# Transposing the FFN's hidden activations with VectorE and DMA in place of TensorE

## The chip, the core and the metric

The kernel runs on one core of a Trainium2 chip, as one program in one launch. The metric is device time in microseconds. The engines are named TensorE (PE in the profile; its weight loads are PEld), VectorE (DVE), ScalarE (ACT), GpSimd (POOL) and SyncE (SP), which issues most DMAs.

## The reference, cut to what matters

256 tokens of 1024 channels in float32 go through a first block (FFN, mixer of chunked attention and pooling, FFN, norm) and then a second block of two attention mixers with layer norms. The change concerns the two FFNs alone:

```python
def swiglu_ffn(x, w_gate, w_up, w_down):
    return (jax.nn.silu(x @ w_gate) * (x @ w_up)) @ w_down
...
x = x + 0.5 * swiglu_ffn(rmsnorm(x, ffn1_norm[l]), ffn1_w_gate[l], ffn1_w_up[l], ffn1_w_down[l])
x = x + hybrid_mixer(...)
x = x + 0.5 * swiglu_ffn(rmsnorm(x, ffn2_norm[l]), ffn2_w_gate[l], ffn2_w_up[l], ffn2_w_down[l])
```

The hidden width is 2816. The product of gate and up, called h here, is the left operand of the product down. TensorE contracts over partitions, so h, which is computed with tokens on the partitions, is needed with hidden channels on the partitions: it has to be transposed.

## The kernel before, in words

There are two tiles t of 128 tokens. Every float32 product is made of three matmuls on operands split into a high and a low part (`mm` at L161, `half` at L213): low x high, high x low, high x high, each 128x128 by up to 512 columns.

Weights come in 236 units of mostly two k-tiles by 512 columns (512 KB). SyncE loads a unit into one of four buffers `raw` (L208), ScalarE casts it to `whi` (L195) and VectorE subtracts to get `wlo` (L196); there are eight buffers of each, so a cast waits until TensorE has finished with the unit eight places earlier. `prefetch` (L184) issues these. `half` does one unit for one tile of tokens: six matmuls for a usual unit.

An FFN (`ffn`, L360 and on) goes over six blocks j of hidden channels, five of 512 and one of 256. In each block, `chunk` (L328) makes the gate product: four units for tile 0, then the same four for tile 1, 24 matmuls each. When a tile is complete, ScalarE makes `th`, a tanh (L383), and VectorE `a` (L385). Then `chunk` makes the up product in the same way, and when a tile is complete VectorE makes `h` (L392). `put_T` (L265) transposes h: one TensorE transpose for each 128x128 block into a PSUM bank `tr` (L177), then ScalarE casts the bank to the high part `hh` (L237) and VectorE subtracts for the low part `hl` (L238). In a block of 512 channels that is four transposes for each tile of tokens. After the six blocks comes the product down: two halves of 512 output columns, eleven units each, unit by unit with both tiles; unit i reads the k-tiles 2i and 2i + 1 of h.

In the first FFN, the first gate product is made by `first_chunk` (L300) with eight units of one k-tile, as the loads arrive.

The order of the work is set in two places. In the code, pieces wait in a heap with a due time in microseconds of TensorE's modelled work: `later` puts a piece in, and `pump`, at the end of every `half`, runs what is due. The h transposes are due `DUE["ffn_T"]` = 2.66 after h. Then the library that builds the program orders each engine's instructions by when it expects their operands, so an instruction can stand ahead of others that the code issues earlier; on the chip each engine runs its list in order.

GpSimd does little in an FFN: the power for the norm (L281), once for each tile, in the first gate product. It issues one DMA in the whole program, the load of `gain` (L1076).

Of the kernel before, what the change touches and what calls it, by code (L numbers as in the profile page):

```python
# [16 lines left out]
P = 128  # L17
# [18 lines left out]
# column blocks of the products with x on the left, in the order in which they are used  # L36
FFN_CH = [(512 * j, min(512, DFF - 512 * j)) for j in range((DFF + 511) // 512)]
MIX_CH = [(1536, 512), (512, 512), (0, 512), (1024, 512)]           # u k q v
FOX_CH = [(1024, 512), (1536, 512), (0, 512), (512, 512),           # k0 k1 q0 q1
          (0, 344), (344, 344), (688, 344),                          # of [f | v]  # L40
          (3080, 512), (3592, 512)]                                  # gate
DSA_CH = [(0, 372), (372, 372),                                      # of [ki | qi | wi | kr | ckv]
          (0, 512), (512, 512), (1768, 512), (2280, 512)]            # q gate


def unit_list():
    """(matrix, first k-tile, k-tiles, first column, columns) in the order of use."""
    u = []

    def block(m, c0, w, k0=0, k1=KT, n=None):  # L50
        n = n or (UK * (512 // w) if 512 % w == 0 else UK)
        for k in range(k0, k1, n):
            u.append((m, k, min(n, k1 - k), c0, w))

    def ffn(i):
        for c0, w in FFN_CH:
            block(f"gate{i}", c0, w, n=1 if i == 1 and c0 == 0 else None)
            block(f"up{i}", c0, w)
        for n in range(2):
            block(f"down{i}", 512 * n, 512, 0, FT)  # L60

    ffn(1)
    for c0, w in MIX_CH:
        block("mix", c0, w)
    for k0 in (4, 0):
        for n in range(2):
            block("mix_out", 512 * n, 512, k0, k0 + 4)
    ffn(2)
    for i, (c0, w) in enumerate(FOX_CH):
        block("fox_fv" if 4 <= i < 7 else "fox", c0, w)  # L70
    for n in range(2):
        block("fox_out", 512 * n, 512)
    for i, (c0, w) in enumerate(DSA_CH):
        block("dsa_idx" if i < 2 else "dsa", c0, w)
    for n in range(2):
        block("dsa_out", 512 * n, 512)
    return u
# [6 lines left out]
# When, in us of the tensor engine's work after what it follows, a piece of work takes its turn.  # L84
DUE = {
    "ffn_T": 2.66,
# [27 lines left out]
class Kern:  # L114
    def __init__(self, ctx, tc, A):
        self.tc, self.nc, self.A, self.ctx = tc, tc.nc, A, ctx
        pool = lambda name, **k: ctx.enter_context(tc.tile_pool(name=name, bufs=1, **k))
        self.cp = pool("const")
        self.wp = pool("w")
        self.xp = pool("x")  # L120
        self.ps = pool("ps", space=bass.MemoryType.PSUM)
        self.now = 0.0
        self.heap, self.fired, self.blocked = [], set(), {}
        self.seq = 0
        self.n_dma = self.n_split = self.used = 0
        self.raw, self.W = {}, {}
        off = 0
        self.off = []
        for (_, _, nk, _, w) in UNITS:
            self.off.append(off)  # L130
            off += P * nk * w

# [5 lines left out]
    def when(self, keys, us, fn):  # L138
        """fn, us after all of the keys are fired."""
        keys = [k for k in keys if k not in self.fired]  # L140
        if not keys:
            self.later(us, fn)
        else:
            self.blocked.setdefault(keys[0], []).append((keys[1:], us, fn))
# [23 lines left out]
    def mm3(self, out, a, b, start, stop, ai=slice(None), bi=slice(None)):  # L168
        """a.T @ b from the parts (hi, lo) of a and b, taken at ai and bi."""
        (ah, al), (bh, bl) = a, b  # L170
        self.mm(out, al[ai], bh[bi], start, False, 1)
        self.mm(out, ah[ai], bl[bi], False, False, 1)
        self.mm(out, ah[ai], bh[bi], False, stop, 1)
# [39 lines left out]
    def half(self, acc, lhs, i, first, last, kbase=0, cols=None):  # L213
        """acc += lhs.T @ unit i, for one tile of tokens; lhs: (hi, lo) of [P, k-tile, P]."""
        if i not in self.W:
            self.prefetch(i + 1 - self.n_split)
        hi, lo = self.W[i]
        _, k0, nk, _, w = UNITS[i]
        xh, xl = lhs
        for k in range(nk):  # L220
            kk = k0 - kbase + k
            c = cols or slice(0, w)
            o = acc[:, 0:c.stop - c.start]
            self.mm(o, xl[:, kk, :], hi[:, k, c], first and k == 0, False, 1)
            self.mm(o, xh[:, kk, :], lo[:, k, c], False, False, 1)
            self.mm(o, xh[:, kk, :], hi[:, k, c], False, last and k == nk - 1, 1)
        self.pump()
# [5 lines left out]
    def split_psum(self, hi, lo, src, scale=None):  # L233
        """hi + lo = src (a PSUM tile), times a column for each of its blocks if scale is given."""
# [15 lines left out]
    def split_scaled(self, dst, src, f):  # L250
        """hi + lo = src f, f a column or a number."""
# [8 lines left out]
    def open_xT(self, t):  # L260
        """After the last product with x[t]: what follows is written to x's operand."""
        self.new_xT(t)
        self.fire((self.stage, "open", t))

    def put_T(self, dst, t, src, k0, n, scale=None):  # L265
        """dst k-tiles k0.. of tile t = transposed blocks of src ([P, n * P])."""
# [5 lines left out]
        self.split_psum(hi[:, k0:k0 + n, :], lo[:, k0:k0 + n, :], v, scale)  # L272

# [12 lines left out]
    def rstd(self, t, src=None, n=D, eps=EPS):  # L286
        """1 / rms of each token of x[t]."""
# [12 lines left out]
    def first_chunk(self, u0, n, pool, gain):  # L300
        """The first block: x's transposes come from memory, a pair of k-tiles at a time."""
# [26 lines left out]
    def chunk(self, u0, n, first_gain=None):  # L328
        """The product of x with one block of columns (units u0 .. u0+n), tile by tile.

        Yields t when tile t is complete. With first_gain the second half of x's transposes
        is made in between, where the vector engines have it ready."""
# [28 lines left out]
    def ffn(self, u, gain, next_gain):  # L361
        nc, tc = self.nc, self.tc
        with tc.tile_pool(name="ffn", bufs=1, reuse_waits="tile") as pool:
            hT = [tuple(pool.tile([P, FT, P], F32R, name=f"h{c}{t}") for c in "hl") for t in range(2)]
            rs = [None, None]
            hr, qr = [None, None], [None, None]
            if u == 0:
                self.xin = pool.tile([P, KT, S], F32, name="xin")
                self.start()
            for j, (c0, w) in enumerate(FFN_CH):  # L370
# [17 lines left out]
                if j == 2 and gain == _GAIN["ffn1"]:  # L388
                    nc.sync.dma_start(out=self.cst[:, P:], in_=self.A["cst"][:, P:])
                for t, acc in self.chunk(u, nu):  # L390
                    h = pool.tile([P, 512], F32, name="h", bufs=3)
                    nc.vector.scalar_tensor_tensor(h[:, :w], a[t][:, :w], qr[t], acc[:, :w],  # L392
                                                   op0=ALU.mult, op1=ALU.mult)
                    self.later(DUE["ffn_T"], lambda t=t, h=h, j=j, w=w: self.put_T(hT[t], t, h, 4 * j, w // P))
                u += nu
            nd = FT // UK
# [18 lines left out]
    def softmax_part(self, pool, s, nh, nk, l, col):  # L415
        """exp(s - max) for nh heads ([P, nh, nk]) in place; row sums into l[:, col..]."""
# [7 lines left out]
    def p_T(self, pool, s, nh, nk, split=False):  # L424
        """Transposes of s: [k, head, k-tile, q], or the parts of [k, k-tile, head, q]."""
# [20 lines left out]
    def mixer(self, u, gain, next_gain):  # L446
        self.stage = "mix"
        nc, tc, A = self.nc, self.tc, self.A
        with tc.tile_pool(name="mix", bufs=1, reuse_waits="tile") as pool:
# [11 lines left out]
            # of the first tile's products whole operands, of the second's the parts  # L461
# [34 lines left out]
            def scores(t, b):  # L496
                """Heads of one half of t: both halves of the array's rows at once, to two banks."""
# [104 lines left out]
    def layer_norm(self, t, o, g, b, out=None):  # L602
        """x[t] = LN(alpha x[t] + o); o: PSUM banks of 512 columns, or of 512, 256, 256."""
# [29 lines left out]
    def silu_gate(self, pool, acc, out, hr):  # L633
        """out = y (1 + tanh(z / 2)) = 2 silu(z) / (z / y); hr: half of z / y, or None for a half."""
# [5 lines left out]
    def out_proj(self, u, after, last=False):  # L640
        """o = og @ w_out, a tile at a time; after(t, (half, half))."""
# [167 lines left out]
    def attend(self, u, pool, gt, hr, scores, pv):  # L809
        """The two gate blocks, with the attention of both tiles between their products."""  # L810
# [25 lines left out]
    def gate_out(self, t, hb, o, l, f, gt):  # L836
        """gt = gt o f / l for four heads, and its transposes into the operand of the product out."""
# [12 lines left out]
    def dsa(self, u, x_gain=None):  # L850
        self.stage = "dsa"
        nc, tc, A = self.nc, self.tc, self.A
        with tc.tile_pool(name="dsa", bufs=1, reuse_waits="tile") as pool:
# [25 lines left out]
            def do_rope(x, n, half, t, off):  # L879
                """x: [P, n, 2 * half + rest], rotated in place."""  # L880
# [192 lines left out]
    def start(self):  # L1073
        """The first loads, those that the first product waits for ahead of the others."""
# [38 lines left out]
def shape_constants():  # L1113
    """Arrays that depend on shapes alone."""
# [29 lines left out]
def layout(inp):  # L1144
    """The inputs, laid out as the kernel reads them."""
# [49 lines left out]
```

## Time and profile before

| | us |
|---|---|
| median of three runs | 741.0 (740.29 to 800.42) |
| span of the profiled execution | 738.3 |
| TensorE busy in it | 723.9 |
| VectorE busy in it | 483.4 |
| ScalarE busy in it | 369.7 |
| first FFN, blocks 1 to 4 (30.4 to 126) | 95.6 |

The profiled execution has a span of 738.3 us from its first to its last instruction. What lies around that span is not listed; the median of the runs is 2.7 us above it. Times in the rows are microseconds from the start of the span unless marked ns. Matmuls are pipelined, so the durations of successive ones overlap: the pace of TensorE is the distance between starts, not the duration. A group's "idle before" names what ended most of an engine's idle time.

### The profile page before, as it was taken

What the parts mean: (1) busy time and instruction counts of PE and PEld (TensorE: products, weight loads), DVE (VectorE), ACT (ScalarE), POOL (GpSimd) and SP (SyncE); (2) the same over time, 40 slices, a digit from 0 to 9 for tenths busy, and PEclk for the clock granted to TensorE, in tenths of its full rate; (3) what the DMA queues carried; (4) which work ended last, traced back from release to release, by engine and by line L of the source; (5) the groups of instructions that cost most, each with busy time, mean ns of one, the idle gap of its engine ahead of it and who ended that gap; (6) DMA issues with size and microseconds to landing.
All of it is one profiled execution on the core that took longest, in us unless ns stands there. A gap on an engine that the chain in (4) does not pass through costs nothing.

```text
span 738.3 us, 9882 instructions
## 1 busy us (share of the span) xinstructions
PE 723.9 (98%) x3696; PEld 606.1 (82%) x3696; DVE 483.4 (65%) x767; ACT 369.7 (50%) x544; POOL 21.7 (3%) x29
## 2 busy tenths in 40 slices
PE   8999999999999999999999999999999999999996
PEld 6788888888888778888888888878987889778985
DVE  5775656545557867655656545565455868998865
ACT  5663544434445745453544434544563635675830
POOL 0000000000002001000000000000000000000001
PEclk9999999999999999999999999999999999999999
DMA  8886556565644335546556565655471317733401
GB/s 259 272 300 214 168 175 222 177 198 181 245 163 148 138 111 175 199 160 211 166 177 219 181 197 177 207 189 153 139 247 39 137 57 262 229 115 115 171 0 58
DMA packets 38257, 128.26 MB, mean 174 GB/s; under 512 B 4402, under 2 KB 5570, under 8 KB 38082
## 3 DMA queue, kind: packets, MB, share of 16 engines
q1 hardware_dynamic: 37890, 127.23, 52.2%
q8 instruction: 29, 0.48, 0.3%
q10 hardware_dynamic: 288, 0.39, 0.1%
q14 instruction: 18, 0.15, 0.1%
q0 software_dynamic: 32, 0.02, 0.0%
HBM read 126.57 MB, written 1.05 MB: 173 GB/s over the span
## 4 chain that ended last, share of the span: by engine, by line
PE 89%; DVE 4%; DMA 4%; ACT 2%; issue 1%; SPq 0%; POOL 0%; DVEq 0%; ACTq 0%
PE mm L162 77%; PE sc L162 6%; PE tr L177 4%; DMA raw<-in_w 2%; DVE wlo L196 1%; DMA row_final_norm<-in_final_norm 1%; PE tr L162 1%; ACT whi L195 1%; DMA x<-in_x 1%; ACT s L421 0%; ACT sq L292 0%; DVE xl L244 0%; DVE sel L958 0%; POOL rs L281 0%; DVE sel L949 0%
## 5 line engine op out<-in xcount | busy, mean ns | idle before, releaser
L196 DVE TENSOR_TENSOR wlo<-raw,whi 128x1024 fp32r<-128x1024 f32 (+3 forms) x236 | 276.4, 1177 | 133.0 <-ACT whi L195 126.7
L195 ACT CAST whi<-raw 128x1024 fp32r<-128x1024 f32 (+3 forms) x236 | 238.4, 1014 | 194.9 <-PE mm L162 170.3
L162 PE MATMUL mm<-whi,xl 128*128 128x512 f32 (+3 forms) x760 | 290.1, 383 | 2.4 <-ACT whi L195 1.2
L162 PE MATMUL mm<-wlo,xh 128*128 128x512 f32 (+3 forms) x760 | 284.2, 374 | 0.4 <-DVE wlo L196 0.4
L162 PE MATMUL mm<-whi,xh 128*128 128x512 f32 (+3 forms) x760 | 283.4, 373 | 0.0
L162 PEld LDWEIGHTS mm<-whi,xl 128*128 128x128 f32 x760 | 143.4, 189 | 25.8 <-ACT whi L195 1.6
L162 PEld LDWEIGHTS mm<-whi,xh 128*128 128x128 f32 x760 | 143.3, 189 | 24.4
L162 PEld LDWEIGHTS mm<-wlo,xh 128*128 128x128 f32 x760 | 143.6, 189 | 23.1 <-DVE wlo L196 1.7
L162 PE MATMUL mm<-whi,hl 128*128 128x512 f32 x176 | 69.0, 392 | 0.0
L162 PE MATMUL mm<-whi,hh 128*128 128x512 f32 x176 | 68.5, 389 | 0.0
L162 PE MATMUL mm<-wlo,hh 128*128 128x512 f32 x176 | 68.5, 389 | 0.0
L162 PEld LDWEIGHTS mm<-whi,hh 128*128 128x128 f32 x176 | 33.0, 188 | 6.9
L162 PEld LDWEIGHTS mm<-wlo,hh 128*128 128x128 f32 x176 | 33.1, 188 | 6.6
L162 PEld LDWEIGHTS mm<-whi,hl 128*128 128x128 f32 x176 | 33.1, 188 | 6.6
L392 DVE SCALAR_TENSOR_TENSOR h<-a,qr,mm 128x512 f32<-128x512 f32 (+1 forms) x24 | 16.8, 698 | 20.4 <-PE mm L162 20.4
L421 ACT ACTIVATE s<-s,nmax 128x128 f32<-128x128 f32 (+1 forms) x48 | 21.3, 445 | 12.3 <-DVE nmax L419 12.3
L237 ACT CAST hh<-tr 128x512 fp32r<-128x512 f32 (+1 forms) x24 | 13.1, 547 | 25.6 <-PE tr L177 25.5
L238 DVE TENSOR_TENSOR hl<-tr,hh 128x512 fp32r<-128x512 f32 (+1 forms) x24 | 15.4, 641 | 16.0 <-ACT hh L237 16.0
L383 ACT ACTIVATE th<-mm,hr 128x512 f32<-128x512 f32 (+1 forms) x24 | 15.7, 653 | 16.2 <-PE mm L162 11.3
L385 DVE SCALAR_TENSOR_TENSOR a<-th,mm 128x512 f32<-128x512 f32 (+1 forms) x24 | 15.3, 638 | 7.8 <-ACT th L383 7.8
L237 ACT CAST xh<-tr 128x512 fp32r<-128x512 f32 x12 | 6.9, 588 | 19.1 <-PE tr L177 19.0
L281 POOL TENSOR_TENSOR rs<-ms,mhalf 128x1 f32<-128x1 f32 x10 | 6.4, 643 | 327.6 <-DVE ms L294 327.6
(222 smaller groups left out, 589.5 us busy)
## 6 DMA issues: line engine op xcount, KB each, us to landing
raw<-in_w SPq DMA_DIRECT2D x208, 512.0 KB, 4.3
raw<-in_w SPq DMA_DIRECT2D x12, 344.0 KB, 3.2
raw<-in_w SPq DMA_DIRECT2D x8, 372.0 KB, 3.9
raw<-in_w SPq DMA_DIRECT2D x8, 256.0 KB, 4.7
x<-in_x SPq DMA_DIRECT2D x2, 512.0 KB, 4.7
B<-in_bias SPq DMA_DIRECT2D x1, 1024.0 KB, 5.5
row_ln_g<-in_ln_g SPq DMA_DIRECT2D x2, 512.0 KB, 6.8
row_ln_b<-in_ln_b SPq DMA_DIRECT2D x2, 512.0 KB, 6.3
```

The source lines that it names most:

```text
L162: self.nc.tensor.matmul(out, a, b, start=start, stop=stop)
L177: self.nc.tensor.transpose(out, a, self.ident[:p, :p])
L195: nc.scalar.copy(hi[:, :m], raw[:, :m])
L196: nc.vector.tensor_sub(lo[:, :m], raw[:, :m], hi[:, :m].bitcast(F32))
L237: nc.scalar.copy(hi, src)
L238: nc.vector.tensor_sub(lo, src, hi.bitcast(F32))
L281: self.nc.gpsimd.tensor_tensor(out, a, self.mhalf[:, 0:1].to_broadcast(list(a.shape)), op=ALU.pow)
L383: nc.scalar.activation(th[:, :w], acc[:, :w], AF.Tanh, scale=hr[t])
L385: nc.vector.scalar_tensor_tensor(a[t][:, :w], th[:, :w], 1.0, acc[:, :w], op0=ALU.add, op1=ALU.mult)
L392: nc.vector.scalar_tensor_tensor(h[:, :w], a[t][:, :w], qr[t], acc[:, :w], op0=ALU.mult, op1=ALU.mult)
L421: nc.scalar.activation(s[:, h, :], s[:, h, :], AF.Exp, bias=m[:, h:h + 1], accum_out=l[:, col + h:col + h + 1])
```

## The change

`put_T` isn't used for h any more. When h of a tile is complete, VectorE transposes it in place of TensorE, in blocks of 32x32: one instruction for each tile of tokens writes `hb`, in which the 32x32 blocks are transposed but stand in the wrong partition groups. After both tiles, `regroup` issues five DMAs from GpSimd: for each of the four groups of 32 partitions a write of hb to a tile `d` in memory (128 KB in runs of 1 KB, for a block of 512 channels), and then one read of d into `hd` (512 KB), in which hidden channels stand on the partitions. `put_h` casts and subtracts from hd as was done from PSUM, for both tiles of tokens together. It is due 6.0 after the end of the block in the heap's microseconds. The buffers of h go from three to two. Comment lines and docstrings also differ; that part is left out.

```diff
 DUE = {
-    "ffn_T": 2.66,
+    "ffn_T": 6.0,
...
         self.ps = pool("ps", space=bass.MemoryType.PSUM)
+        self.dp = pool("d", space=bass.MemoryType.DRAM)
...
+    def regroup(self, dst, src):
+        m = src.shape[2]
+        d = self.dp.tile([4, 4, 32, 256], F32, name="d", tag="d", bufs=4)[:, :, :, 0:m]
+        for a in range(4):
+            self.nc.gpsimd.dma_start(out=d[a].rearrange("b i m -> i b m"), in_=src[32 * a:32 * a + 32])
+        self.nc.gpsimd.dma_start(out=dst, in_=d.rearrange("a b i m -> (b i) a m"))
...
+            def put_h(j, n, hd):
+                for t in range(2):
+                    hi, lo = (d[:, 4 * j:4 * j + n, :].rearrange("p c (a j) -> p c a j", a=4) for d in hT[t])
+                    v = hd[:, :, t * 32 * n:(t + 1) * 32 * n].rearrange("p a (c j) -> p c a j", c=n)
+                    self.split_psum(hi, lo, v)
...
+                n = w // P
+                hb = pool.tile([P, 4, 256], F32, name="hb", bufs=2)
                 for t, acc in self.chunk(u, nu):
-                    h = pool.tile([P, 512], F32, name="h", bufs=3)
+                    h = pool.tile([P, 512], F32, name="h", bufs=2)
                     nc.vector.scalar_tensor_tensor(h[:, :w], a[t][:, :w], qr[t], acc[:, :w],
                                                    op0=ALU.mult, op1=ALU.mult)
-                    self.later(DUE["ffn_T"], lambda t=t, h=h, j=j, w=w: self.put_T(hT[t], t, h, 4 * j, w // P))
+                    nc.vector.transpose(
+                        hb[:, :, t * 32 * n:(t + 1) * 32 * n].rearrange("p b (c j) -> p b c j", c=n),
+                        h[:, :w].rearrange("p (c b j) -> p b c j", c=n, b=4))
                 u += nu
+                hd = pool.tile([P, 4, 256], F32, name="hd", bufs=2)
+                self.regroup(hd[:, :, 0:64 * n], hb[:, :, 0:64 * n])
+                self.later(DUE["ffn_T"], lambda j=j, n=n, hd=hd: put_h(j, n, hd))
```

## Rows read from the trace of the kernel before

**Rows 1.** The page, busy us, share of the span and instructions of each engine.

```profile
PE 723.9 (98%) x3696; PEld 606.1 (82%) x3696; DVE 483.4 (65%) x767; ACT 369.7 (50%) x544; POOL 21.7 (3%) x29
```

**Rows 2.** Windows: stretch, length; busy of each engine (instructions); granted clock; DMA share; GB/s.

```profile
40.00:60.00 20.00, 20.00 (x94) 16.57 (x93) 15.25 (x15) 11.15 (x13) 0.00 (x0) 1.00 0.86 289
...
30.40:126.00 95.60, 95.60 (x449) 79.42 (x448) 63.93 (x66) 50.49 (x57) 0.00 (x0) 1.00 0.63 209
```

**Rows 3.** Waits of TensorE, longest first: us in all, times, longest.

```profile
PE tr L177 <- DVE y L891: 1.3, 1, 1.3
...
PE mm L162 <- ACT whi L195: 1.2, 1, 1.2
```

**Rows 4.** ScalarE's timeline in a steady block: start, us, instruction [idle before].

```profile
61.55 0.69 ACT L383 ACTIVATE th<-mm,hr 128x512 f32<-128x512 f32 x1 [0.81 <-PE mm L162]
...
84.30 0.69 ACT L383 ACTIVATE th<-mm,hr 128x512 f32<-128x512 f32 x1 [0.81 <-PE mm L162]
85.68 1.05 ACT L195 CAST whi<-raw 128x1024 fp32r<-128x1024 f32 x1 [0.69 <-PE mm L162]
```

**Rows 5.** VectorE's timeline in the same stretch.

```profile
72.46 0.75 DVE L392 SCALAR_TENSOR_TENSOR h<-a,qr,mm 128x512 f32<-128x512 f32 x1 [2.56 <-PE mm L162]
...
79.36 0.74 DVE L392 SCALAR_TENSOR_TENSOR h<-a,qr,mm 128x512 f32<-128x512 f32 x1
...
86.77 3.95 DVE L196 TENSOR_TENSOR wlo<-raw,whi 128x1024 fp32r<-128x1024 f32 x3 [1.06 <-ACT whi L195]
...
95.21 0.75 DVE L392 SCALAR_TENSOR_TENSOR h<-a,qr,mm 128x512 f32<-128x512 f32 x1 [2.56 <-PE mm L162]
```

**Rows 6.** Groups by line and shape: count, busy us, mean ns, idle before.

```profile
L196 DVE TENSOR_TENSOR wlo<-raw,whi 128x1024 fp32r<-128x1024 f32 x208 | 253.4, 1223 | 117.6 <-ACT whi L195 111.4
...
L392 DVE SCALAR_TENSOR_TENSOR h<-a,qr,mm 128x512 f32<-128x512 f32 x20 | 14.8, 742 | 20.0 <-PE mm L162 20.0
L238 DVE TENSOR_TENSOR hl<-tr,hh 128x512 fp32r<-128x512 f32 x20 | 13.7, 686 | 16.0 <-ACT hh L237 16.0
...
L177 PE MATMUL tr<-cst,h 128*128 128x128 f32 x88 | 13.5, 271 | 0.0
...
L237 ACT CAST hh<-tr 128x512 fp32r<-128x512 f32 x20 | 11.7, 583 | 24.5 <-PE tr L177 24.4
```

**Rows 7.** TensorE's timeline at one group of four transposes.

```profile
76.34 0.60 PE L177 MATMUL tr<-cst,h 128*128 128x128 f32 x4
76.70 0.48 PE L162 MATMUL mm<-whi,xl 128*128 128x512 f32 x1
77.01 0.40 PE L162 MATMUL mm<-wlo,xh 128*128 128x512 f32 x1
```

**Rows 8.** DMA: the weight queue's share; issues with size and us to landing.

```profile
q1 hardware_dynamic: 37890, 127.23, 52.2%
...
raw<-in_w SPq DMA_DIRECT2D x208, 512.0 KB, 4.3
...
row_ln_g<-in_ln_g SPq DMA_DIRECT2D x2, 512.0 KB, 6.8
...
out<-x SPq DMA_DIRECT2D x2, 256.0 KB, 2.0
...
gain<-in_gain POOLq DMA_DIRECT2D x1, 19.0 KB, 3.4
```

**Rows 9.** GpSimd's timeline: its one DMA issue.

```profile
1.23 0.71 POOL L1076 DMA_DIRECT2D gain<-in_gain  x1 [0.79 <-POOLq L1187]
```

**Rows 10.** ScalarE's timeline in the first product and in the first block.

```profile
15.56 1.06 ACT L292 ACTIVATE sq<-x 128x1024 bf16<-128x1024 f32 x1 [1.20 <-DMA x<-in_x]
...
41.04 1.05 ACT L195 CAST whi<-raw 128x1024 fp32r<-128x1024 f32 x1 [0.43 <-DMA raw<-in_w]
```

**Rows 11.** VectorE's timeline in the first blocks.

```profile
34.33 0.74 DVE L392 SCALAR_TENSOR_TENSOR h<-a,qr,mm 128x512 f32<-128x512 f32 x1
...
49.79 0.74 DVE L392 SCALAR_TENSOR_TENSOR h<-a,qr,mm 128x512 f32<-128x512 f32 x1
```

## The prediction

> **What bounds the kernel now.** I read the page's busy times first. TensorE is busy for 723.9 of 738.3 us, VectorE for 65% of the span and ScalarE for 50% [rows 1]. The second view is its granted clock, stretch by stretch: 1.00, the 2.4 GHz level, in both stretches of the first FFN [rows 2], so there is no slow clock to win back. The third is who TensorE waited for: the longest entry is 1.3 us, and the longest for weights 1.2 us [rows 3]. So TensorE's own stream of instructions is the limit, and whatever leaves it shortens the run, as long as no new wait comes in.
>
> The fourth view is one FFN block in the steady part, on the two vector engines. From the tanh at 61.55 to the h at 72.46 TensorE does 48 matmuls and no transpose: 10.91 us, 0.227 us a matmul. From that h to the tanh at 84.30 it does 48 matmuls and eight transposes: 11.84 us [rows 4, 5]. All three follow the end of a product directly.
>
> **What goes.** The difference, 0.93 us for eight, prices a transpose at 0.116 us on TensorE's path. There are 88 in the two FFNs [rows 6] (22 k-tiles, two tiles of tokens, twice): 88 x 0.116 = 10.2 us. Their busy sum is 13.5 us [rows 6], which counts overlap twice and is the upper end. For a lower end I take the gap in which a group stands, 0.36 us from the first transpose to the next matmul [rows 7], or 22 x 0.36 = 7.9 us; the matmul after that one starts 0.31 us later instead of 0.227, so the 10.2 is nearer. The evacuation doesn't go: the 24 casts hh and 24 subtractions hl stay, with memory-fed tiles in SBUF as their source. I price them as before, at 0.583 and 0.686 us [rows 6]; for a source in SBUF the subtraction may take 0.61, half of the 1.223 us of twice as many columns, and the cast as much less. Neither is on TensorE's path.
>
> **What comes on VectorE.** 24 block transposes. No row shows one; the nearest are hl (0.686), h (0.742) and, from above, the subtraction of 1024 columns (1.223) [rows 6]. I take 0.74, because it has the same number of columns: about 1.5 us in a block of 22 us, in a stage where VectorE works 63.9 of 95.6 us [rows 2]. It is hidden behind TensorE and costs 0; at the upper end it is 2.4 us a block, hidden too. What it does cost is delay of the chain below.
>
> **What comes on the DMA queues.** Each block issues five DMAs from GpSimd: four of 128 KB to memory, and one of 512 KB back that waits for all four. That is 12 x 5 = 60 issues and, with the half-wide last blocks, 2 x 2 x 2.88 = 11.5 MB. The weight queue's 127.23 MB take 52.2% of the span, 3.03 us of all engines per MB [rows 8], so a full block adds 3.2 us (1.05 MB) in 22, on a share of 0.63 [rows 2]: hidden. Bounds: nothing, or twice that for the shorter pieces (1 KB), 0.92 of the engines, still under 1. GpSimd has nothing else queued behind the waiting read: it does no instruction in that stretch [rows 2].
>
> **How late the regrouped tile is.** L is the time from the last block transpose to the landing of the read. An issue from GpSimd took 0.71 us [rows 9]; that transfer landed after 3.4 us, a 512 KB load after 4.3 us (median) or 6.8 at worst, and a store of 256 KB after 2.0 us [rows 8]. Central: three issues (2.1), the fourth write's landing (3.4), a hand-over of the order of an issue (0.7) and the read with its own issue (4.3 + 0.7): 11.2 us. Lower: 2.1 + 2.0 + 4.3 = 8.4. Upper, if every write lands before the next is issued: 4 x 3.4 + 6.8 = 20.4. I take 11.2; each of its terms is a row.
>
> The due time of 6 us only says where put_h stands in the order, about the middle of the next gate product, ahead of its last weight casts. So ScalarE waits there for the tile. Behind it on ScalarE are the weight casts, then the tanh; on VectorE their subtractions and a. TensorE waits for those. How much can be late? The cast at 85.68 is followed by its subtraction at 86.77, ending at 88.0 [rows 4, 5]. Its unit is first used when the up product ends, 5.9 us after the h at 95.21 (24 matmuls and four transposes), at 100.9: 12.9 us of slack. With put_h ahead of it, the cast starts at 79.36 + 0.74 (h) + 0.74 (transpose) + L + 2 x 0.58 = 82.0 + L. With L = 11.2 that is 7.5 us late, hidden with 5.4 us left; TensorE would wait from L = 16.6 on. The tile itself isn't needed before the down product; the last block's is used there by its last unit, some 27 us on.
>
> The one thin place is the first block of the first FFN, where the weights are still catching up: the DMA share is 0.86 from 40 to 60 us [rows 2]. There the cast at 41.04 is the fourth unit of the next up product [rows 10]. Its first use is 6 matmuls before the h at 49.79 [rows 11], at 49.79 - 0.3 - 1.36 = 48.1, or 47.2 without the eight transposes. The h at 34.33 [rows 11] comes 0.5 us earlier, with four transposes gone ahead of it, and the regrouped tile at 34.33 - 0.5 + 1.48 + 11.2 = 46.5; two casts, the unit's cast and its subtraction end at 46.5 + 1.17 + 1.05 + 1.3 = 50.0. If put_h stands ahead of that cast, as the code has it, TensorE waits 2.8 us. But the program's builder moves instructions: the square at 15.56 stands ahead of weight casts that the code issues earlier [rows 10]. So the bounds are 0 and 2.8, and I take the middle, 1.4.
>
> **The sum.** 738.3 - 10.2 + 1.4 = 729.5 us of span. The median of the runs shown, 741.0, lies 2.7 us above this span, and I take that as the part around it: 732.2 us, a gain of 1.2%. A measurement of this kernel tells about 2% from no change.
>
> Two rules of the Trainium skill bear on this. Its page VectorE: DVE Perf Modes (Rules for kernel authors) says to transpose 128x128 on TensorE where a PSUM destination will do. By that the move brings nothing, and the time would be C's below; the rows speak against it, since here the 0.116 us lie on the engine that sets the end and VectorE has room. Its page DMA: Bandwidth & Descriptors (Anatomy of one DMA, the GpSimd path) gives about 2.0 us plus the bytes over 436 GB/s for a DMA; my estimate of L by that page is 2.1 + 2.3 + 3.2 = 7.6 us, which would leave out the 1.4 and give 730.8 us. No row shows such a transfer of 128 or 512 KB.
>
> **Rivals.**
> A, the gain is eaten at the start. The two first regroups (2 x 3.2 us of DMA time) fall where the weight queue has least to spare, and the thin cushion of 5 us goes with it: 2.8 for the late cast plus up to 6.4 for late loads, 9.2 in place of 1.4: 740 us. For it: the share of 0.86 and the casts that wait for loads there [rows 2, 10]. Against: only units used before the buffers are full are thin, the steady blocks have 12.9 us, and the late loads would have to fall on those few.
> B, slower: ScalarE stands at put_h longer than the weights last. At L = 20.4 the cast is 16.7 us late in every block and TensorE waits 3.8 us in seven blocks (four in each FFN are followed by a full gate product, less the first one), and 2.8 + 9.2 = 12.0 in the first: 38.6 - 10.2 = +28.4, 769 us. TensorE's gain is lost from 8 L = 10.2 + 7 x 16.6 + 8.4, L = 16.9, and 2% slower begins near L = 18.7. For it: no row shows a write of 1 KB pieces from 32 partitions, nor a read queued behind it. Against: the one GpSimd transfer landed in 3.4 us beside the opening loads.
> C, the change doesn't do what it says: the matmuls around the transposes stretch and the path keeps its length, 741 us. Against: the 0.227 us pace without them is seen in the same rows.
>
> **How the numbers follow.** The forecast (path shorter by the transposes, chain hidden but for a few us) gets 0.72, A 0.12, B 0.12, C 0.04. The forecast's own range is 741.0 - 13.5 = 727.5 to 741.0 - 7.9 + 2.8 = 735.9. To hold 8 in 10 I reach over A and C to 743, and B stays outside: 728 to 743. Faster by over 2% means under 726.2, a gain of 14.8 us, more than the transposes' busy sum: 0.02. Slower by over 2% means over 755.8, B at L above 18.7 and something unforeseen: 0.11. The rest, 0.87, is within 2%.
>
> **What would show it.** Right: no tr<-cst,h group; 88 matmul records fewer on TensorE; gate and up products both at 10.9 us for 48 matmuls; 24 block transposes near 0.74 us; some 6.8 MB written to memory instead of 1.05; a wait of ScalarE's put_h cast on the read of about 6 us a block (the tile lands 13 us after the up product's end, and the cast is due after five halves of 1.36 us), and no more than 3 us of TensorE waiting for weights in the first 60 us. Wrong: TensorE waiting for whi or wlo in every block (B), the read landing over 16.6 us after the last block transpose, or a matmul pace above 0.227 us.

## The result, and the profile after

| | before | after |
|---|---|---|
| median, us | 741.4 (740.29 to 800.42, 4 runs) | 730.53 (729.38 to 731.16, 4 runs) |
| profiled execution, us | | 731.11 |
| its span, us | 738.3 | 729.3 |

The ratio is 0.9868, 95% interval 0.9845 to 0.989: about 1.3% faster, which is within the 2% that the chances went by. The forecast was 732.2, in a range of 728 to 743. One high run among those of before, 800.42 us, was left out of the ratio.

The first look goes to the page of the changed kernel: busy us by engine, the GpSimd DMA queue (packets, MB, share), and the traffic with memory.

```profile
PE 713.9 (98%) x3608; PEld 597.6 (82%) x3608; DVE 493.7 (68%) x791; ACT 366.6 (50%) x544; POOL 58.2 (8%) x89
...
q0 software_dynamic: 3808, 11.56, 4.6%
...
HBM read 132.34 MB, written 6.82 MB: 191 GB/s over the span
```

Against [rows 1] TensorE has 88 records fewer, VectorE 24 more, GpSimd 60 more. 11.56 MB take 4.6% of the span, 33.5 us: 2.9 us per MB, where 3.03 was used. The same windows as in [rows 2] follow.

```profile
40.00:60.00 20.00, 20.00 (x90) 16.57 (x89) 15.34 (x17) 11.53 (x13) 0.97 (x2) 1.00 0.92 317
30.40:126.00 95.60, 95.60 (x452) 80.42 (x451) 66.80 (x73) 48.74 (x56) 11.88 (x20) 1.00 0.73 250
```

The DMA share rose from 0.86 to 0.92 and from 0.63 to 0.73. TensorE is busy in the whole of both stretches and its granted clock stays at 1.00, the 2.4 GHz level.

ScalarE's timeline, start and us, around the first put_h and in the blocks that [rows 4] shows of before:

```profile
39.86 1.05 ACT L196 CAST whi<-raw 128x1024 fp32r<-128x1024 f32 x1 [1.35 <-DMA raw<-in_w]
...
46.01 1.98 ACT L196 CAST whi<-raw 128x1024 fp32r<-128x1024 f32 x2
48.73 1.14 ACT L238 CAST hh<-hd 128x512 fp32r<-128x512 f32 x2 [0.73 <-DMA hd<-d]
...
59.15 0.69 ACT L400 ACTIVATE th<-mm,hr 128x512 f32<-128x512 f32 x1 [2.09 <-PE mm L163]
...
80.91 0.69 ACT L400 ACTIVATE th<-mm,hr 128x512 f32<-128x512 f32 x1 [2.89 <-PE mm L163]
...
86.94 1.04 ACT L196 CAST whi<-raw 128x1024 fp32r<-128x1024 f32 x1
95.72 1.14 ACT L238 CAST hh<-hd 128x512 fp32r<-128x512 f32 x2 [7.74 <-DMA hd<-d]
96.77 2.00 ACT L196 CAST whi<-raw 128x1024 fp32r<-128x1024 f32 x2
```

From tanh to tanh a block took 84.30 - 61.55 = 22.75 us; now it takes 80.91 - 59.15 = 21.76, 96 matmuls at 0.227 us. The difference, 0.99 us for eight transposes, is 0.124 us each. The casts of put_h (L238) wait 7.74 us for the regrouped tile. They stand behind all four weight casts that are made during the gate product, and at that place ScalarE waited for TensorE before the change as well, 5.17 us, as its timeline in the kernel before shows:

```profile
73.82 1.05 ACT L195 CAST whi<-raw 128x1024 fp32r<-128x1024 f32 x1 [5.17 <-PE mm L162]
```

VectorE and GpSimd of the changed kernel in the block from 80.91 on:

```profile
81.53 0.70 DVE L413 STREAM_TRANSPOSE hb<-h 128x512 f32<-128x512 f32 x1
...
96.37 1.29 DVE L239 TENSOR_TENSOR hl<-hd,hh 128x512 fp32r<-128x512 f32 x2 [7.14 <-ACT hh L238]
97.58 0.74 DVE L411 SCALAR_TENSOR_TENSOR h<-a,qr,mm 128x512 f32<-128x512 f32 x1
...
82.52 2.19 POOL L281 DMA_DIRECT2D d<-hb  x4 [16.29 <-DVE hb L413]
89.64 0.76 POOL L282 DMA_DIRECT2D hd<-d  x1 [4.92 <-DMA d<-hb]
```

Here the chain can be read off. The last block transpose ends at 82.23; four writes are issued until 84.71; the read waits 4.92 us for them and lands just before the cast at 95.72. So L, the time from the last block transpose to the landed read, is some 13.5 us. Over the ten full blocks it was 12.8 to 14.6 (the two narrow ones 12.6 and 16.5). Then VectorE, which stood at put_h's subtraction, makes at 97.58 the h that TensorE had finished by 80.91 + 48 x 0.227 = 91.8: it is 5.8 us late, and so is what hangs on it. The groups (h, its block transpose, hl and hh) and the DMA issues of the page (KB, us to landing):

```profile
L411 DVE SCALAR_TENSOR_TENSOR h<-a,qr,mm 128x512 f32<-128x512 f32 x20 | 14.8, 742 | 2.3 <-PE mm L163 2.3
L413 DVE STREAM_TRANSPOSE hb<-h 128x512 f32<-128x512 f32 x20 | 14.2, 708 | 0.3
L239 DVE TENSOR_TENSOR hl<-hd,hh 128x512 fp32r<-128x512 f32 x20 | 12.9, 689 | 54.5 <-ACT hh L238 54.5
L238 ACT CAST hh<-hd 128x512 fp32r<-128x512 f32 x20 | 11.4, 618 | 60.9 <-DMA hd<-d 60.9
...
d<-hb POOLq DMA_DIRECT2D x40, 128.0 KB, 4.3
hd<-d POOLq DMA_DIRECT2D x10, 512.0 KB, 6.2
```

Two waits in the trace bear on the rest: of TensorE (us, times, longest) one that is new, for x, the sum with the residual, which it transposes next; and of ScalarE the stand at put_h.

```profile
PE tr L178 <- DVE x L433: 0.9, 1, 0.9
...
ACT hh L238 <- DMA hd<-d: 70.8, 12, 8.2
```

**Where the time went.** I set the start of each matmul after against that of the same one before. It is 0.44 us earlier ahead of the first group of transposes that is gone (start-up), 5.82 behind the last group of the first FFN, 5.78 at the second FFN and 11.17 behind its last group: 5.38 + 5.39 = 10.8 us from the two FFNs. About 1.3 is lost again in that product down, at TensorE's wait for x (above) and the transposes right behind it; 0.2 come back after it. The last stores are issued 734.55 - 724.48 = 10.07 us earlier. Yet the span is only 9.0 us shorter. The difference is at the end of the program, in GpSimd's last wait for its queue to empty (count, then min/median/max in ns), first after, then before:

```profile
L1215 POOLq DRAIN  x3: 40/102/6105, 722.4 to 729.0; - x3
```

```profile
L1191 POOLq DRAIN  x3: 34/89/1183, 732.5 to 738.0; - x3
```

Its longest drain takes 6.1 us in place of 1.18 and ends after the stores have landed. From the last store's issue to the end it is 729.3 - 724.48 = 4.8 us, before it was 3.75.

### The profile page after: what moved, and what is told of

It is laid out like the page before. It is cut to its first block, busy times and chain, and to the rows that moved or that the text cites. A ratio compares the mean times of both kernels' runs of the same rounds, so it can differ in the third digit from the quotient of the medians.

```text
span 729.3 us, 9860 instructions
## 1 busy us (share of the span) xinstructions
PE 713.9 (98%) x3608; PEld 597.6 (82%) x3608; DVE 493.7 (68%) x791; ACT 366.6 (50%) x544; POOL 58.2 (8%) x89
## 3 DMA queue, kind: packets, MB, share of 16 engines
q0 software_dynamic: 3808, 11.56, 4.6%
## 4 chain that ended last, share of the span: by engine, by line
PE 73%; DMA 11%; DVE 9%; issue 2%; ACT 2%; POOL 2%; SPq 0%; DVEq 0%; POOLq 0%; ACTq 0%
PE mm L163 63%; PE sc L163 6%; DVE wlo L197 4%; DMA raw<-in_w 3%; PE tr L178 3%; DMA hd<-d 3%; DMA d<-hb 2%; DMA rope<-in_rope 1%; POOL hrs L291 1%; ACT whi L196 1%; DMA row_final_norm<-in_final_norm 1%; PE tr L163 1%; POOL d L281 1%; DMA x<-in_x 1%; ACT s L445 0%
## 5 line engine op out<-in xcount | busy, mean ns | idle before, releaser
L196 ACT CAST whi<-raw 128x1024 fp32r<-128x1024 f32 (+3 forms) x236 | 235.5, 1013 | 133.0 <-PE mm L163 82.5
L239 DVE TENSOR_TENSOR hl<-hd,hh 128x512 fp32r<-128x512 f32 (+1 forms) x24 | 14.5, 644 | 62.4 <-ACT hh L238 62.4
L238 ACT CAST hh<-hd 128x512 fp32r<-128x512 f32 (+1 forms) x24 | 12.8, 582 | 70.8 <-DMA hd<-d 70.8
L281 POOL DMA_DIRECT2D d<-hb x48 | 26.4, 556 | 148.2 <-DVE hb L413 148.0
L445 ACT ACTIVATE s<-s,nmax 128x128 f32<-128x128 f32 (+1 forms) x48 | 21.3, 446 | 12.8 <-DVE nmax L443 12.7
```

What stands on the lines that cost most here:

```text
L196: nc.scalar.copy(hi[:, :m], raw[:, :m])
L238: nc.scalar.copy(hi, src)
L239: nc.vector.tensor_sub(lo, src, hi.bitcast(F32))
L281: self.nc.gpsimd.dma_start(out=d[a].rearrange("b i m -> i b m"), in_=src[32 * a:32 * a + 32])
L445: nc.scalar.activation(s[:, h, :], s[:, h, :], AF.Exp, bias=m[:, h:h + 1], accum_out=l[:, col + h:col + h + 1])
```

## The experiments

Each ratio is against the kernel before, run beside it on the same chip. Where the expectations number their theories, theory one is the forecast's account.

**What the regrouping costs.** One kernel without the DMAs, so that h reaches the product down with its 32x32 blocks in the wrong places.

```diff
-                hd = pool.tile([P, 4, 256], F32, name="hd", bufs=2)
-                self.regroup(hd[:, :, 0:64 * n], hb[:, :, 0:64 * n])
+                hd = hb
```

> The changed kernel without its five DMAs a block: put_h casts straight from hb, so h reaches the product down with its 32x32 blocks in the wrong places; all else is kept. Theory (what the regrouping costs is 1.2 us of TensorE in the second FFN's product down, through a late add of the residual, and 1.0 us in GpSimd's last drain; the rest is hidden): the casts from hb wait for nothing, the drain is back at about 1.2 us, no wait of the x transposes on L433, span 729.3 - 2.2 = 727.1 us. Rival (the add is late because VectorE has 24 transposes more, and the drain is long for another reason): span within 0.5 of 729.3.

Measured: 728.4 us (726.51 to 731.39), ratio 0.9835 (0.9796 to 0.9873), span 726.9. The wait for x at L433 is gone and the drain is 1.18 us again. So the twelve regroups cost about 2 us by the medians (the intervals of the two ratios overlap), and hiding them better can bring little more than that. In this kernel the builder also sets put_h some seven weight casts further forward, so the 2 us are the price of the DMAs and of the later place together.

**Doing the transposes twice.** The 88 transposes are put back on TensorE, their result unread, beside the new way; the buffers of h go back to three.

```diff
+                    self.later(2.66, lambda h=h, n=n: self.only_tr(h, n))
```

> The changed kernel with TensorE's 88 transposes of h put back as well, into a PSUM bank that nothing reads. Theory (TensorE's stream is the limit, and a group of four costs it 0.49 us): 22 x 0.49 = 10.8 us more, span 740.1 us, the last work as late as in the kernel before. Rival (the gain came in part from the evacuation that now reads SBUF and is off the banks): less than 8 us more.

Measured: 741.44 us (739.57 to 745.51, 10 runs), ratio 1.0013 (0.9994 to 1.0033), where the changed kernel has 0.9868. The difference, 0.0145 of some 740 us, is 10.7 us (10.9 between the medians), and 88 x 0.124 is 10.9. TensorE's path does carry 0.12 us for each transpose: in the profiled execution its matmuls run 3.2 to 3.3 us behind those of the kernel before from 60 to 465 us, through both FFNs, so the transposes cost what they cost before. That execution, 743.7 us of span, also shows where those 3 us come from, in TensorE's timeline at one late group of transposes:

```profile
55.19 0.66 PE L178 MATMUL tr<-cst,h 128*128 128x128 f32 x4 [2.95 <-DVE h L416]
...
56.15 0.40 PE L163 MATMUL mm<-whi,xh 128*128 128x512 f32 x1
...
57.56 0.63 PE L163 MATMUL mm<-whi,xl 128*128 128x512 f32 x1
57.99 0.63 PE L163 MATMUL mm<-wlo,xh 128*128 128x512 f32 x1
```

After a wait of 2.95 us the distance between matmuls goes from 0.23 to 0.43 us for 3.4 us: the 1.2 GHz level. This wait was paid again in clock.

**A later place for put_h.** The due time goes from 6 to 18.

```diff
-    "ffn_T": 6.0,
+    "ffn_T": 18.0,
```

> The changed kernel with put_h due 18 instead of 6 us after the block, so that ScalarE reaches its casts when the regrouped tile is there. Theory (ScalarE's hold at the last block's put_h makes the weight casts pile up and the add of the residual late): the holds on hd, 70.8 us in all, fall below 15 us, and TensorE's wait on L433 goes: span 728.1 us, drain as before the run at about 6 us. Rival (the loads, slowed by the regrouping, are what is late): holds gone, but the wait on L433 stays and the span is 729.3.

Measured: 730.76 us (729.97 to 732.68), ratio 0.9867 (0.9842 to 0.9892). ScalarE's stand at put_h was 61.5 us, not under 15: the builder left put_h where it was, behind the four casts of the gate product. Between 6 and 18 the due time doesn't set that place, so what a later place would bring no run shows. The wait for x was gone in that execution, but so it was in a repeat of the changed kernel:

> The changed kernel itself once more, as the base for the others of this call. Theory (the 1.2 us of TensorE lost in the second FFN's product down come from one late landing, 16.5 us after the last block transpose where the other blocks have about 13.6): the loss varies from execution to execution, the last drain on GpSimd stays near 6.1 us, and the span is 728 to 730. Rival (the loss belongs to the order of the instructions): TensorE waits for L433 again, by about 0.9 us.

Measured: 730.09 us (728.33 to 731.6), ratio 0.9867 (0.9845 to 0.989); no wait at L433, with L of the last block 12.3 in place of 16.5 (13.4 in the run above). In these three executions that wait comes and goes with one late transfer. Its span of 729.8 is no shorter for that, since TensorE waited longer for y (L711), behind the second FFN, instead:

```profile
PE tr L178 <- ACT y L711: 2.0, 1, 2.0
```

Behind that wait matmuls are 0.43 us apart for 3.4 us. The drain is 6.1 us in all three.

**The same DMAs from SyncE.** The five issues of a regroup move from GpSimd to SyncE's queue.

```diff
-            self.nc.gpsimd.dma_start(out=d[a].rearrange("b i m -> i b m"), in_=src[32 * a:32 * a + 32])
-        self.nc.gpsimd.dma_start(out=dst, in_=d.rearrange("a b i m -> (b i) a m"))
+            self.nc.sync.dma_start(out=d[a].rearrange("b i m -> i b m"), in_=src[32 * a:32 * a + 32])
+        self.nc.sync.dma_start(out=dst, in_=d.rearrange("a b i m -> (b i) a m"))
```

> The changed kernel with the five DMAs of a block issued from SyncE, where the weight loads are issued too, and not from GpSimd. Theory (GpSimd's last drain grows by 0.08 us for each DMA that it issued, from 1.18 with one to 6.1 with 61 and 8.1 with 85 of them, and only its end beyond the last store counts): the drain is back at 1.2 us and 1.0 us of the span goes; the read waits for the writes in front of the weight loads, 4 to 6 us a block, which the slack of 8 us covers: span 728 us or less. Rival (the loads that stand behind the read come late): TensorE waits for whi or wlo in most blocks, span over 735.

Measured: 728.11 us (727.53 to 729.51), ratio 0.9844 (0.9826 to 0.9862), span 727.7. The end of the program and the stand at put_h in its trace:

```profile
L1215 POOLq DRAIN  x3: 34/93/1183, 721.6 to 727.5; - x3
```

```profile
ACT hh L238 <- DMA hd<-d: 20.1, 5, 5.5
```

The drain is what it was before, and from the last store's issue (723.72) to the end it is 4.0 us. The stand at put_h falls from 70.8 to 20.1. Not the queue alone has changed: in the first FFN the builder also sets put_h one to three weight casts further forward. The price stands in the weights: VectorE finishes some of them only 2 to 3 us ahead of their use, where the changed kernel has 7.7 or more in its steady blocks; SyncE now stands 13.3 us in all for block transposes and 12.4 for writes to land, with loads of weights queued behind. The changed kernel, run beside it, took 730.09, 2.0 us more; the intervals of the two ratios overlap, so the gain over the changed kernel is likely, but 0.3% is at the edge of what these runs tell. The drain accounts for 0.8 us of it (4.8 us from the last store to the end against 4.0); the rest lies in waits of TensorE that differ between executions, as the one for y above. The Trainium skill, DMA: Bandwidth & Descriptors (SWDGE vs HWDGE vs iDMA), says that plain transfers belong on SyncE's or ScalarE's queue; the medians point the same way. Both edits at once:

> The same with put_h due 18 us after the block. Theory (the builder places put_h by when it expects the tile, and the due time does little, as in the run with 18 us and GpSimd's queue): within 1 us of the run on SyncE with 6. Rival (on SyncE the later place helps the loads): 2 us or more faster than it.

Measured: 728.19 us (727.81 to 730.41), ratio 0.9849 (0.9828 to 0.9869): the same.

**How late may the tile be?** Rival B said that TensorE waits for weights from L = 16.6 on. Two copies more through memory make L 22.5 to 28.7; the builder sets put_h two or three weight casts further back for it.

```diff
+        for k in range(2):
+            e = self.dp.tile([4, 4, 32, 256], F32, name=f"e{k}", tag=f"e{k}", bufs=4)[:, :, :, 0:m]
+            self.nc.gpsimd.dma_start(out=e.rearrange("a b i m -> (a b i) m"), in_=d.rearrange("a b i m -> (a b i) m"))
+            d = e
```

> The changed kernel with two copies from memory to memory between the four writes and the read, so that the regrouped tile comes some 10 to 13 us later (L about 24 to 26 us instead of 13.5). Theory one (the prediction's working: put_h stands ahead of the weight casts, and TensorE waits for all that L exceeds 16.6): 7 to 9 us in each of seven blocks and more in the first, 780 us or more. Theory two (the builder puts put_h behind the casts of the gate product, where ScalarE would wait for TensorE anyway, with 7.7 to 8.6 us of slack left at L = 13.5): TensorE waits for 2 to 5 us a block, 745 to 770 us. Theory three (the builder reckons with the longer chain and puts put_h later still): 729 to 733 us, the last block's tile alone being late at the product down.

Measured: 798.0 us (797.54 to 803.11), ratio 1.0786 (1.0747 to 1.0826), span 795.8, granted clock 0.963. Whom TensorE waited for:

```profile
PE mm L163 <- DVE hl L239: 17.8, 4, 7.5
PE mm L163 <- DVE h L415: 16.6, 2, 8.5
PE mm L163 <- ACT whi L196: 9.0, 4, 3.6
PE mm L163 <- DVE wlo L197: 4.5, 4, 1.2
```

The size is as theory one has it: 66.5 us more span than the changed kernel. But only 13.5 us of the 47.9 in these lines are waits for weights. 17.8 are for hl in the products down and 16.6 for h. Behind waits TensorE runs on at the 1.2 GHz level (granted clock 0.50 to 0.52), in seven stretches of 2.9 to 7.1 us, 33.7 us in all; at half the pace that is about 17 us more. The rest, 2 us, is the end of the program, where the drain takes 8.06 us. One copy more (`range(1)`), with L of 17.4 to 19.4, and of 21.4 to 22.3 in the very first block and the two narrow ones, lies near the threshold:

> The changed kernel with one copy from memory to memory between the writes and the read: L near 18.5 us. Theory one (the prediction's working, TensorE waits for what L exceeds 16.6): 1.9 us in each of eight blocks, 15 us or more with the first block's, span 744 or more. Theory two (with two copies TensorE waited 3.8 us a block at L = 23.5, so the limit is near 19.7): no wait in the steady blocks, the clock stays at its upper level, drain about 7.1 us, span 730 to 734.

Measured: 759.76 us (757.63 to 762.17), ratio 1.0279 (1.0244 to 1.0315), span 755.8, granted clock 0.980. Neither account gets all of it: the amount lies on theory one's side, the wait isn't its. TensorE's waits, then VectorE's timeline, TensorE's, and the window behind that wait (us; busy of PE, PEld, DVE, ACT, POOL; granted clock, DMA share, GB/s):

```profile
PE mm L163 <- DVE h L415: 14.3, 2, 8.1
...
PE mm L163 <- ACT whi L196: 2.1, 2, 1.5
```

```profile
131.92 1.29 DVE L239 TENSOR_TENSOR hl<-hd,hh 128x512 fp32r<-128x512 f32 x2 [7.51 <-ACT hh L238]
133.38 3.50 DVE L197 TENSOR_TENSOR wlo<-raw,whi 128x1024 fp32r<-128x1024 f32 x3 [0.17 <-ACT whi L196]
136.80 0.74 DVE L415 SCALAR_TENSOR_TENSOR h<-a,qr,mm 128x512 f32<-128x512 f32 x1
...
137.59 0.58 PE L163 MATMUL mm<-whi,xl 128*128 128x256 f32 x1 [6.17 <-DVE h L415]
```

```profile
137.00:143.00 6.00, 5.41 (x26) 5.37 (x27) 5.80 (x9) 3.51 (x4) 2.19 (x4) 0.56 0.96 308
```

The narrow sixth block is half as wide, so TensorE reaches its up product sooner. That product needs the PSUM bank that the fifth block's h reads, and that h stands on VectorE behind put_h's subtraction and three weights. TensorE waits 6.17 us, and then the granted clock is 0.56. In the changed kernel the same h ends at 125.04 and the bank is needed at 127.42: a margin of 2.4 us.

To see whether the bank is the cause, the last kernel gives the narrow block's two products PSUM banks of their own, still with one copy more.

```diff
-            accs[t] = self.bank("mm")
+            accs[t] = self.bank(tag)
...
-                    self.chunk(u, ng, gain if j == 0 else None)
+                    self.chunk(u, ng, gain if j == 0 else None, "tr" if j == 5 else "mm")
...
-                for t, acc in self.chunk(u, nu):
+                for t, acc in self.chunk(u, nu, tag="sc" if j == 5 else "mm"):
```

> The kernel with one more copy through memory, in which the two products up of the narrow sixth block take PSUM banks of their own (the two banks of tr for the gate product, the two of sc for the other). Theory: what TensorE waited for in the narrow block was a PSUM bank, held by the previous block's h, whose instruction stood on VectorE behind put_h's subtraction, and the half clock came after that wait. With banks of their own for those products the 14.3 us of waits for h go, and with them most of the stretches at half clock (about 8 us): span 733 to 742. Rival: VectorE's stand delays everything that TensorE needs from it, so the wait only moves on to the weights or to the next product down: over 750.

Measured: 760.98 us (756.29 to 764.07), ratio 1.0257 (1.0194 to 1.0319), span 760.1: the rival's side. TensorE's waits, its timeline in the first product down, and GpSimd's:

```profile
PE mm L163 <- DVE hl L239: 12.9, 4, 4.4
PE mm L163 <- ACT whi L196: 4.2, 2, 2.4
```

```profile
161.52 0.50 PE L163 MATMUL mm<-whi,hl 128*128 128x512 f32 x1 [3.19 <-DVE hl L239]
...
172.81 0.69 PE L163 MATMUL mm<-whi,hl 128*128 128x512 f32 x1 [3.91 <-DVE hl L239]
...
154.63 0.80 POOL L286 DMA_DIRECT2D hd<-e  x1 [4.43 <-DMA e<-d]
155.42 2.19 POOL L281 DMA_DIRECT2D d<-hb  x4
```

The wait for h is gone, 14.3 us to none, so the bank was what TensorE stood at. But no time comes of it: 12.9 us of waits for hl stand in the products down, each long one with matmuls at 0.43 us behind it. The fifth block's h is as late as it was, its tile lands late, and the sixth block's writes, ready at 148.4, stand on GpSimd behind the fifth's read until 155.42. A late tile delays VectorE's h, and through it the bank, the next regroup and the product down; take one of these away and TensorE stops at the next.

## Why the prediction held, point by point

- **The transposes.** 0.116 us each was predicted and 10.2 us in all. The block's period gives 0.124, the matmul starts 10.8 us over both FFNs, and putting the transposes back cost 10.7: the mechanism is right, and the size 5% low. The upper figure from their busy sum, 13.5, was too high for the reason named, and the 7.9 too low. Rival C is out: the pace stayed at 0.227 us.
- **VectorE.** 24 block transposes at 0.708 us, 0.74 predicted. The subtraction from SBUF takes 0.689, as from PSUM, and the cast 0.618 against 0.583 [rows 6]: the lower price considered for a source in SBUF didn't come. The Trainium skill's advice to use TensorE for 128x128 (VectorE: DVE Perf Modes, Rules for kernel authors) doesn't hold here, where TensorE is the bound; its price on that path is the 10.7 us just named.
- **L.** 11.2 was predicted; 13.5 us was read in a steady block, inside the bounds 8.4 to 20.4. Mis-sized were the landings: 4.3 us for a write of 128 KB against 3.4, and 6.2 for a read of 512 KB against 4.3. The Trainium skill's formula (DMA: Bandwidth & Descriptors, Anatomy of one DMA) gave 2.3 and 3.2 us; beside the weight loads neither is met. The 730.8 us that the forecast gave by that page lie near the result, but not by its L of 7.6: the 1.4 that it left out fell away for another reason (below). The prediction had nothing queued behind the waiting read; in both narrow blocks the writes stand behind the fifth block's read, so that they start about 1 us after the last block transpose instead of 0.3, and with one more copy 7 us after it (above).
- **Where put_h stands.** The forecast put ScalarE's wait ahead of the last weight casts of the gate product, and on that ground the next cast 7.5 us late, with 5.4 us left. It stands behind them, at a place where ScalarE waited 5.17 us anyway. The stand of 5.9 us a block (70.8 over 12) agrees with the "about 6" predicted, yet by luck, from two errors of opposite sign. In the block shown the tile lands 20.2 us after the up product's end at 75.5, where 13 was forecast, and ScalarE reaches put_h 12.5 us after it, where 6.8 was. Of the 7 us by which the tile is later, 2.3 are L. The rest is what the prediction missed, the second hold: h of the next block stands on VectorE behind put_h.
- **The first block.** 1.4 us was added, the middle of 0 and 2.8. It is 0: put_h's casts at 48.73 stand behind all casts of the next up product (the last at 39.86) and of the gate product after it (46.01), which the builder moved ahead. TensorE waited 0.4 us for whi in the whole run. With it rival A falls: the DMA share there reached 0.92 and no load was late enough to show.
- **The end.** The sum had 738.3 - 10.2 + 1.4 = 729.5 us of span. The traces have 738.3 - 10.8 for the transposes, 0.4 less at start-up, 1.3 more for the late x, 0.2 less behind it, and 1.1 more for GpSimd's longer drain: 729.3. The late x and the drain were not in the sum, and stand about where the 1.4 and the low price of the transposes stood. That the span came out within 0.2 us is the luck of these terms. Around the span lie 731.11 - 729.3 = 1.8 us, not 2.7: the span of before was that of an execution faster than the median. So of the 1.7 us by which the forecast is high, 0.2 are the span, 0.9 the part around it, and 0.6 the profiled execution's own distance from the median.
- **Rival B.** At L = 13.5 it isn't reached. One copy more, with L near 18, gave 2.6 to 2.8% slower; by B's own sum L = 18 costs 7 x 1.4 + 9.6 - 10.2 = 9.2 us (seven blocks beyond 16.6, the first beyond 8.4, less the transposes), 1.2%. So it saw about where the loss begins, and priced it too low. Its mechanism was wrong in part: it saw ScalarE and the weights alone. The runs show VectorE's h, the PSUM banks, the product down and the clock as the larger part.

## What to carry to other kernels

Where TensorE sets the end, a transpose on it costs its place in the stream, here 0.12 us for 128x128 in float32, and moving it to an engine with room pays that, less what the new way costs, here about 2 us. A round trip through memory costs little as long as the instruction that consumes it stands where its engine would wait anyway: look for everything queued behind that instruction, on both vector engines, not only for the operand one thinks of. Near such a threshold count the waits and what the clock takes after them; here put_h's stand of up to 8 us on two engines cost little at L = 13.5, and one copy more cost 26 us of span.

## What the runs showed of the hardware that was not expected

- **GpSimd's drain at the end** grows with the DMAs that it issued in the program: 1.18 us with 1, 6.10 with 61, and with 73 and 85 as below, so 0.082 us for each. It shows in the time only where it outlasts the last store. In the changed kernel the store lands 5.0 us after the drain's start; no run has a count between 1 and 61.

```profile
L1219 POOLq DRAIN  x3: 40/102/7085, 747.9 to 755.5; - x3
```

```profile
L1219 POOLq DRAIN  x3: 40/93/8065, 786.9 to 795.5; - x3
```

- **A wait is often paid twice.** At waits of 1.5 to 8.5 us in TensorE-bound stages the granted clock fell to the 1.2 GHz level, for 3.4 to 10.2 us (part of it in the wait itself), with matmuls 0.43 us apart instead of 0.227 behind it. It did so at the 1.95 us for y in the repeat of the changed kernel, and did not at two waits of 2.0 us in the kernel with two copies.
